# First four k tiles in smaller loads from two queues, last products in two column halves, output in quarter rows

## The chip, the cores and the metric

The kernel runs on one core of one Trainium2 chip. The metric is device time in microseconds (us) of one launch, from the program's start to its end; lower is better. Times are medians of several runs. The profile is one further execution taken by the hardware profiler, with times counted from the start of its span.

Engines in what follows: PE is TensorE (matrix products), PEld its weight loads, DVE is VectorE, ACT is ScalarE, POOL is GpSimd, SP is SyncE, which here only issues transfers. A "q" behind an engine (SPq, ACTq) means its instruction sequencer, for instance when it issues a DMA.

## The reference

Two pre-norm residual layers over a stream of 256 tokens by 2048 features, float32, batch 1, and a final RMSNorm:

```python
def reference(x, norm_mix, norm_ffn, norm_final, w_in_even, w_out_even, swa_sinks,
              mlstm_b_i, mlstm_b_f, mlstm_head_gain, w_in_odd, fox_b_f, w_out_odd,
              w_gate, w_up, w_down):
    h = x
    for layer in range(DEPTH):          # DEPTH = 2
        j = layer // 2
        xn = rms_norm(h, norm_mix[layer])
        if layer % 2 == 0:
            mix = swa_mlstm_mixer(xn, w_in_even[j], w_out_even[j], swa_sinks[j],
                                  mlstm_b_i[j], mlstm_b_f[j], mlstm_head_gain[j])
        else:
            mix = forgetting_attention_mixer(xn, w_in_odd[j], fox_b_f[j], w_out_odd[j])
        h = h + mix.astype(h.dtype)
        h = h + swiglu(rms_norm(h, norm_ffn[layer]), w_gate[layer], w_up[layer], w_down[layer])
    return rms_norm(h, norm_final)

def rms_norm(x, g):
    xf = x.astype(jnp.float32)
    y = xf * lax.rsqrt(jnp.mean(xf * xf, axis=-1, keepdims=True) + RMS_EPS)
    return (y * g.astype(jnp.float32)).astype(x.dtype)

def swiglu(xn, w_gate, w_up, w_down):
    return (jax.nn.silu(xn @ w_gate) * (xn @ w_up)) @ w_down
```

Nearly all the work is matrix products of the 256 tokens with float32 weights. The change touches the first of these products (`xn @ w_in_even`, from its first tiles on) and the last (`... @ w_down` of the second layer, its last 512 output columns) with the final norm behind it.

## The kernel before

**A product.** Features lie on the partitions: D = 2048 features are KT = 16 k tiles of P = 128. The 256 tokens are two row tiles, t = 0 and 1, of 128. Output columns go in groups of NB = 512. Each float32 operand is split into a high part of reduced precision and the rest, and one product is three matmuls: high by high, high by the weights' rest, x's rest by high (L204 to L206). The x side (128 x 128) is the stationary operand, the weights (128 x 512) stream past it.

**Weights.** `load_raw` (L115) loads CK = 2 k tiles of 512 columns, 512 KB, in one DMA on SP into one of four `raw` buffers. `split_chunk` (L169) makes `hi` on ACT (L176) and `lo = raw - hi` on DVE (L177). `gemm` (L190) walks the k tiles of one column group: for each k, both row tiles, three matmuls each. In the last chunk group (`skew` chunks of 2 k tiles) it sorts by row tile, so that t = 0 ends first and its output work runs under the products of t = 1.

**The start** (L103 to L135 and L697 to L705). ACT issues a 32 KB load of the norm gains `gT` (L111); a one-element copy (L105) makes it load its function table. SP issues x, which is stored transposed as `xt`, into `xc` in five pieces (L127: k 0-1, 2-3, 4-7, 8-11, 12-15) with the first four weight loads between them. Meanwhile PE runs WARM = 3 rounds of four 128 x 128 float32 products on a constant (L135). Then, in four steps of four k tiles, ACT makes `xh = xc * gain` (L700), DVE makes the rest `xl` (L701), and `gemm` takes those k tiles into `acc0`.

**The end** (L643 to L648 and L1249 to L1272). In the last pass of the second layer the column groups n = 2 and n = 3 of `w_down` go through `gemm`, n = 3 with skew = 3, so that its last six k tiles run all for t = 0 and then all for t = 1: 18 matmuls of 512 columns for each. `finish` adds the sums to `h`, takes the sum of squares on ACT (L1256), and for n = 3 the mean on DVE (L1265) and the power -1/2 on POOL (L1266), scales the row tile (ACT the first 1024 columns, L1267; DVE the others, L1268 and L1269) and SP writes it out in two halves of 1024 columns (L1272).

**What sets the order.** A scheduler in the compiler places each engine's instructions by a simulated timeline; `tc.issue_after` adds an order by hand. Every DMA of SP and ACT takes one of eight completion semaphores (DMAHW0 to DMAHW7) in turn, and a DMA is issued only when the earlier one on its semaphore has landed. SP issues in program order, so a waiting DMA holds back those behind it.

Of the kernel before, what the change touches and what calls it, by code (L numbers as in the profile page):

```python
# [35 lines left out]
WARM = 3  # L36
# [28 lines left out]
def trunk(  # L65
# [45 lines left out]
    nc.scalar.dma_start(gT, gains)  # L111

# [19 lines left out]
    for _ in range(WARM):  # L132
        pw = pm.tile([P, 4, P], F32, tag="pm", name="pw")
        for i in range(4):
            nc.tensor.matmul(pw[:, i, :], ones, ones, start=True, stop=True)  # L135
# [26 lines left out]
    last_split = [None]  # L162
    last_mul = [None]

    def load_chunk(w, k0, c0, n):
        raw = ahead.pop(0) if ahead else load_raw(w, k0, c0, n)
        return split_chunk(raw, n)

    def split_chunk(raw, n):  # L169
        hi = wp.tile([P, CK, NB], F32R, tag="hi", name="hi")  # L170
        lo = wp.tile([P, CK, NB], F32R, tag="lo", name="lo")
        with ExitStack() as order:
            if behind[0]:
                order.enter_context(tc.issue_after(behind[0].ins))
                behind[0] = None
            latest[0] = nc.scalar.copy(hi[:, :, 0:n], raw[:, :, 0:n])  # L176
        nc.vector.tensor_tensor(  # L177
            out=lo[:, :, 0:n], in0=raw[:, :, 0:n], in1=hi[:, :, 0:n].bitcast(F32), op=ALU.subtract
        )
        return hi, lo  # L180
# [9 lines left out]
    def gemm(acc, lhs, w, c0, n, k_from, k_to, k_all, skew=1):  # L190
        k0 = k_from
        while k0 < k_to:
            last = k_to == k_all and k0 + skew * CK >= k_all
            chunks = [load_chunk(w, kc, c0, n) for kc in range(k0, k_all if last else k0 + CK, CK)]
            order = [(i, t) for i in range(len(chunks) * CK) for t in range(NT)]
            if last:
                order.sort(key=lambda it: it[1])
            for i, t in order:
                k = k0 + i
                hi, lo = (c[:, i % CK, 0:n] for c in chunks[i // CK])  # L200
                ah, al = lhs(k)
                ts = slice(t * P, (t + 1) * P)
                o = acc[t][:, 0:n]
                nc.tensor.matmul(o, ah[:, ts], hi, start=(k == 0), stop=False)  # L204
                nc.tensor.matmul(o, ah[:, ts], lo, start=False, stop=False)  # L205
                last_mm[0] = nc.tensor.matmul(o, al[:, ts], hi, start=False, stop=(k == k_all - 1))  # L206
            k0 += len(chunks) * CK
# [360 lines left out]
    def ffn(layer, fp, room, pending, sx, sd, key, idx_next=None, key_next=None, finish=None, then=None):  # L568
# [8 lines left out]
        for part, (g0, g1) in enumerate(zip(PARTS, PARTS[1:])):  # L577
# [64 lines left out]
            for n0 in (0, 2):  # L642
                if end and idx_next is None and n0 == 2:  # L643
                    for n in (2, 3):
                        acc = new_acc()
                        gemm(acc, m_of, wd, n * NB, NB, 0, nk, nk, skew=3 if n == 3 else 1)
                        close(acc, n)
                    continue  # L648
# [49 lines left out]
    for n in range(4):  # L698
        for k in range(4 * n, 4 * n + 4):
            nc.scalar.mul(xh[:, k, :], xc[:, k, :], gT[:, k : k + 1])  # L700
# [4 lines left out]
        gemm(acc0, x_of, wi, OFF_KS, NB, 4 * n, 4 * n + 4, KT)  # L705
# [540 lines left out]
    fs = cp.tile([P, NT, 4], F32, name="fs")  # L1246
    ft = cp.tile([P, 3, NT], F32, name="ft")

    def finish(acc, n, gf):  # L1249
        ns = slice(n * NB, (n + 1) * NB)  # L1250
        gn_ = gf[n // CK][:, n % CK, :]
        for t in range(NT):
            o = h[:, t, ns]
            nc.vector.tensor_tensor(out=o, in0=acc[t], in1=o, op=ALU.add)
            junk = sm.tile([P, NB], BF16, tag="junk", name="junk", bufs=1)
            nc.scalar.activation(junk, o, AF.Square, accum_out=fs[:, t, n : n + 1])  # L1256
# [8 lines left out]
            nc.vector.tensor_scalar(mean, fs[:, t, 3:4], 1.0 / D, part, op0=ALU.mult, op1=ALU.add)  # L1265
            nc.gpsimd.tensor_tensor(out=rs, in0=mean, in1=mhalf[:, 0:1], op=ALU.pow)  # L1266
            nc.scalar.mul(h[:, t, 0 : 2 * NB], h[:, t, 0 : 2 * NB], rs)  # L1267
            nc.vector.tensor_scalar(h[:, t, 2 * NB : 3 * NB], h[:, t, 2 * NB : 3 * NB], rs, None, op0=ALU.mult)  # L1268
            nc.vector.scalar_tensor_tensor(out=o, in0=o, scalar=rs, in1=gn_, op0=ALU.mult, op1=ALU.mult)  # L1269
            for half in (1, 0):  # L1270
                hs = slice(half * 2 * NB, (half + 1) * 2 * NB)
                nc.sync.dma_start(ov[:, t, hs], h[:, t, hs])  # L1272
# [51 lines left out]
```

## Time and profile before

| | us |
|---|---|
| median of 3 runs | 2087.18 |
| the three runs | 2086.15, 2087.18, 2089.94 |
| the profiled execution, its whole time | 2087.4 |
| its span | 2085.6 |
| PE busy within the span | 2074.6 |
| DVE busy | 1803.8 |
| ACT busy | 1378.9 |

The span is what the profiler recorded between the first and the last event; 1.8 us of the profiled execution lie around it. A row of a timeline gives the start in us, the length in us, the engine, the line of the kernel, the operation, the tiles (out<-in) and how many instructions were merged; what stands in brackets is the engine's idle time ahead of it and what ended it. Matmuls are pipelined, so one that is listed with 0.39 us follows the one before it after 0.23 us.

### The profile page before, as it was taken

How to read it: one execution, taken by the hardware profiler on the slowest of the kernel's cores; microseconds unless marked ns; L12 is line 12 of the kernel's file. 1: busy time of each engine (PE TensorE's matmuls, PEld its weight loads, DVE VectorE, ACT ScalarE, POOL GpSimd, SP SyncE). 2: the span in 40 equal slices, each digit the busy share in tenths (PEclk: the TensorE clock that was granted, in tenths of full speed). 3: DMA queues.
4: the chain of work that ended last, by engine and by line, in shares of the span. 5: the costliest groups of instructions: out<-in, count | busy, mean ns of one | idle time of the engine just before them, and what ended most of it. 6: DMA issues, size and time to landing. Idle time of an engine off the chain costs nothing.

```text
span 2085.6 us, 26737 instructions
## 1 busy us (share of the span) xinstructions
PE 2074.6 (99%) x9486; PEld 1723.5 (83%) x9486; DVE 1803.8 (86%) x2396; ACT 1378.9 (66%) x1733; POOL 51.6 (2%) x70
## 2 busy tenths in 40 slices
PE   9999999999999999999999999999999999999998
PEld 7888888888888888888888888888888888888886
DVE  6788868999999998998799776679999999999995
ACT  6577568666567656767867676687666567556763
POOL 2110000000000000000020000000000000000000
PEclk9999999999999999999999999999999999999999
DMA  9446767766676667666687675677767576757663
GB/s 332 125 142 184 247 193 228 240 198 205 211 228 214 214 195 220 212 220 176 200 261 207 199 212 169 197 231 231 231 194 229 187 230 201 239 177 226 219 205 125
DMA packets 308661, 435.61 MB, mean 209 GB/s; under 512 B 106272, under 2 KB 114480, under 8 KB 308528
## 3 DMA queue, kind: packets, MB, share of 16 engines
q1 hardware_dynamic: 306768, 428.10, 65.3%
q0 software_dynamic: 1616, 5.78, 0.9%
q8 instruction: 74, 1.21, 0.2%
q14 instruction: 59, 0.48, 0.1%
q10 hardware_dynamic: 144, 0.03, 0.0%
HBM read 408.67 MB, written 2.11 MB: 197 GB/s over the span
## 4 chain that ended last, share of the span: by engine, by line
PE 98%; DMA 1%; DVE 0%; ACT 0%; issue 0%; POOLq 0%; POOL 0%; SPq 0%; DVEq 0%; ACTq 0%
PE acc L427 20%; PE acc L428 20%; PE acc L429 20%; PE acc L205 5%; PE acc L206 5%; PE acc L204 5%; PE prod L427 5%; PE prod L428 5%; PE prod L429 5%; PE vacc L206 1%; PE vacc L204 1%; PE vacc L205 1%; PE p L333 1%; PE po L386 1%; PE pp L378 0%
## 5 line engine op out<-in xcount | busy, mean ns | idle before, releaser
L176 ACT CAST hi<-raw 128x1024 fp32r<-128x1024 f32 (+1 forms) x664 | 674.0, 1030 | 406.0 <-PE acc L429 239.7
L177 DVE TENSOR_TENSOR lo<-raw,hi 128x1024 fp32r<-128x1024 f32 (+1 forms) x664 | 786.0, 1199 | 139.3 <-ACT hi L176 137.5
L428 PE MATMUL acc<-lo,xh 128*128 128x512 f32 x1204 | 469.1, 390 | 0.0
L429 PE MATMUL acc<-hi,xl 128*128 128x512 f32 x1204 | 465.1, 389 | 0.0
L427 PE MATMUL acc<-hi,xh 128*128 128x512 f32 x1204 | 462.9, 390 | 0.2 <-DVE u L562 0.2
L427 PEld LDWEIGHTS acc<-hi,xh 128*128 128x128 f32 x1204 | 226.3, 188 | 48.2 <-DVE u L562 0.6
L429 PEld LDWEIGHTS acc<-hi,xl 128*128 128x128 f32 x1204 | 226.4, 188 | 47.2
L428 PEld LDWEIGHTS acc<-lo,xh 128*128 128x128 f32 x1204 | 226.4, 188 | 47.0
L428 PE MATMUL acc<-lo,mh 128*128 128x512 f32 x444 | 172.7, 389 | 0.0
L429 PE MATMUL acc<-hi,ml 128*128 128x512 f32 x444 | 171.4, 389 | 0.0
L427 PE MATMUL acc<-hi,mh 128*128 128x512 f32 x444 | 169.3, 389 | 0.0
L302 ACT CAST ht<-raw 128x1024 fp32r<-128x1024 f32 x94 | 98.7, 1050 | 56.4 <-DVE raw L542 19.0
L205 PE MATMUL acc<-lo,mh 128*128 128x512 f32 x320 | 125.8, 393 | 0.0
L302 ACT CAST ht<-t 128x1024 fp32r<-128x1024 f32 x94 | 98.9, 1052 | 40.3 <-PE prod L429 27.3
L204 PE MATMUL acc<-hi,mh 128*128 128x512 f32 x320 | 125.4, 396 | 0.0
L206 PE MATMUL acc<-hi,ml 128*128 128x512 f32 x320 | 124.1, 391 | 0.0
L303 DVE TENSOR_TENSOR lt<-raw,ht 128x1024 fp32r<-128x1024 f32 x94 | 114.9, 1222 | 4.3 <-ACT ht L302 4.0
L303 DVE TENSOR_TENSOR lt<-t,ht 128x1024 fp32r<-128x1024 f32 x94 | 114.9, 1222 | 1.6 <-ACT ht L302 1.3
L302 ACT CAST hi<-raw 128x512 fp32r<-128x512 f32 x112 | 69.2, 618 | 59.5 <-PE acc L429 47.3
L429 PEld LDWEIGHTS acc<-hi,ml 128*128 128x128 f32 x444 | 83.4, 188 | 17.3
L427 PEld LDWEIGHTS acc<-hi,mh 128*128 128x128 f32 x444 | 83.4, 188 | 17.3
L428 PEld LDWEIGHTS acc<-lo,mh 128*128 128x128 f32 x444 | 83.3, 188 | 17.3
(370 smaller groups left out, 3588.5 us busy)
## 6 DMA issues: line engine op xcount, KB each, us to landing
raw<-in_w_gate_dram SPq DMA_DIRECT2D x176, 512.0 KB, 4.6
raw<-in_w_up_dram SPq DMA_DIRECT2D x176, 512.0 KB, 4.7
raw<-in_w_down_dram SPq DMA_DIRECT2D x176, 512.0 KB, 5.0
raw<-in_w_in_odd_dram SPq DMA_DIRECT2D x88, 512.0 KB, 4.9
raw<-in_w_in_even_dram SPq DMA_DIRECT2D x64, 512.0 KB, 4.8
raw<-in_w_out_even_dram SPq DMA_DIRECT2D x32, 512.0 KB, 4.5
raw<-in_w_out_odd_dram SPq DMA_DIRECT2D x32, 512.0 KB, 4.7
raw<-in_w_in_odd_dram SPq DMA_DIRECT2D x8, 272.0 KB, 3.3
```

The lines of the kernel that those rows point to most:

```text
L176: latest[0] = nc.scalar.copy(hi[:, :, 0:n], raw[:, :, 0:n])
L177: nc.vector.tensor_tensor(out=lo[:, :, 0:n], in0=raw[:, :, 0:n], in1=hi[:, :, 0:n].bitcast(F32), op=ALU.subtract)
L204: nc.tensor.matmul(o, ah[:, ts], hi, start=(k == 0), stop=False)
L205: nc.tensor.matmul(o, ah[:, ts], lo, start=False, stop=False)
L206: last_mm[0] = nc.tensor.matmul(o, al[:, ts], hi, start=False, stop=(k == k_all - 1))
L302: last_split[0] = nc.scalar.copy(dst_h, src)
L303: nc.vector.tensor_tensor(out=dst_l, in0=src, in1=dst_h.bitcast(F32), op=ALU.subtract)
L333: nc.tensor.matmul(p1[:, jj, :], q_of(j, 1), k_of(j), start=True, stop=True)
L386: nc.tensor.matmul(po, v_of(j, 0), t0[:, j, :], start=True, stop=False)
L427: nc.tensor.matmul(o, ah, hi, start=start, stop=False)
L428: nc.tensor.matmul(o, ah, lo, start=False, stop=False)
L429: nc.tensor.matmul(o, al, hi, start=False, stop=stop)
```

## The change

At the start: the first four k tiles of weights come as four loads of 256 KB, one for each k tile, ahead of everything else on SP; x of k 0 and k 1 comes as two loads of 128 KB issued by ACT; x of k 2-3 and then of k 4-5 and 6-7 in 256 KB loads on SP. `split_chunk` splits those first weights one k tile at a time, and x is scaled in steps of 2, 2, 2, 2, 4 and 4 k tiles, with each step's scaling ordered behind the cast before it. The constant products ahead (WARM) go from 12 to 10.

At the end: for n = 3, row tile t = 1, the products of the last six k tiles go into two new PSUM tiles of 256 columns, first all for the left half, then all for the right, 36 matmuls of 256 columns in place of 18 of 512. What t = 1 had gathered before is added to `h` on its own, each half is added and squared by itself, and the row tile is scaled and written in four quarters of 512 columns, three on SP and one on ACT.

```diff
-WARM = 3
+WARM = 10
...
     nc.scalar.dma_start(gT, gains)
+    for k in range(CK):
+        nc.scalar.dma_start(xc[:, k, :], xt[:, k, :])
...
-    for k0, k1, ks in ((0, 2, (0,)), (2, 4, (2,)), (4, 8, (4, 6)), (8, 12, ()), (12, 16, ())):
+    firsts = []
+
+    def load_first(k0):
+        raw = wr.tile([P, CK, NB], F32, tag="raw", name="raw", bufs=4)
+        for a in range(CK):
+            k = k0 + a
+            load[0] = nc.sync.dma_start(raw[:, a, :], wi[k * P : (k + 1) * P, OFF_KS : OFF_KS + NB])
+        firsts.append(raw)
+        ahead.append(raw)
+
+    load_first(0)
+    nc.sync.dma_start(xc[:, 2:4, :], xt[:, 2:4, :])
+    load_first(2)
+    for k0, k1, ks in ((4, 6, (4,)), (6, 8, (6,)), (8, 12, ()), (12, 16, ())):
         nc.sync.dma_start(xc[:, k0:k1, :], xt[:, k0:k1, :])
         ahead += [load_raw(wi, k, OFF_KS, NB) for k in ks]
...
-    for _ in range(WARM):
-        pw = pm.tile([P, 4, P], F32, tag="pm", name="pw")
-        for i in range(4):
-            nc.tensor.matmul(pw[:, i, :], ones, ones, start=True, stop=True)
+    pw = pm.tile([P, 4, P], F32, tag="pm", name="pw")
+    for i in range(WARM):
+        nc.tensor.matmul(pw[:, i % 4, :], ones, ones, start=True, stop=True)
...
+        for a in range(parts):
+            ks = slice(a * CK // parts, (a + 1) * CK // parts)
+            with ExitStack() as order:
+                if parts > 1:
+                    order.enter_context(tc.issue_after(xh_made[len(xh_made) - parts + a].ins))
...
+                latest[0] = nc.scalar.copy(hi[:, ks, 0:n], raw[:, ks, 0:n])
+            nc.vector.tensor_tensor(
+                out=lo[:, ks, 0:n], in0=raw[:, ks, 0:n], in1=hi[:, ks, 0:n].bitcast(F32), op=ALU.subtract
+            )
...
+            if last and halves:
+                head = [it for it in order if it[1] < NT - 1]
+                end = [it[0] for it in order if it[1] == NT - 1]
+                order = head + [
+                    (i, NT - 1, half, a * n // 2, (a + 1) * n // 2, k0) for a, half in enumerate(halves) for i in end
+                ]
...
-    for n in range(4):
-        for k in range(4 * n, 4 * n + 4):
-            nc.scalar.mul(xh[:, k, :], xc[:, k, :], gT[:, k : k + 1])
+    for k0, k1 in ((0, 2), (2, 4), (4, 6), (6, 8), (8, 12), (12, 16)):
+        with ExitStack() as order:
+            if k0:
+                order.enter_context(tc.issue_after(latest[0].ins))
+            for k in range(k0, k1):
+                xh_made.append(nc.scalar.mul(xh[:, k, :], xc[:, k, :], gT[:, k : k + 1]))
...
+            pieces = 2 if halves and t == NT - 1 else 1
+            if pieces == 2:
+                o = h[:, t, n * NB : (n + 1) * NB]
+                nc.vector.tensor_tensor(out=o, in0=acc[t], in1=o, op=ALU.add)
+            for a in range(pieces):
+                w = NB // pieces
+                o = h[:, t, n * NB + a * w : n * NB + (a + 1) * w]
+                nc.vector.tensor_tensor(out=o, in0=halves[a] if pieces == 2 else acc[t], in1=o, op=ALU.add)
+                junk = sm.tile([P, NB], BF16, tag="junk", name="junk", bufs=1)
+                nc.scalar.activation(junk[:, 0:w], o, AF.Square, accum_out=fs[:, t, n + a : n + a + 1])
+                if n == 3:
+                    dst = mean if a == pieces - 1 else part
+                    nc.vector.tensor_scalar(dst, fs[:, t, 3 + a : 4 + a], 1.0 / D, part, op0=ALU.mult, op1=ALU.add)
...
-            nc.scalar.mul(h[:, t, 0 : 2 * NB], h[:, t, 0 : 2 * NB], rs)
-            nc.vector.tensor_scalar(h[:, t, 2 * NB : 3 * NB], h[:, t, 2 * NB : 3 * NB], rs, None, op0=ALU.mult)
-            nc.vector.scalar_tensor_tensor(out=o, in0=o, scalar=rs, in1=gn_, op0=ALU.mult, op1=ALU.mult)
-            for half in (1, 0):
-                hs = slice(half * 2 * NB, (half + 1) * 2 * NB)
-                nc.sync.dma_start(ov[:, t, hs], h[:, t, hs])
+            q = [h[:, t, a * NB : (a + 1) * NB] for a in range(4)]
+            qo = [ov[:, t, a * NB : (a + 1) * NB] for a in range(4)]
+            nc.scalar.mul(q[0], q[0], rs)
+            nc.vector.tensor_scalar(q[2], q[2], rs, None, op0=ALU.mult)
+            nc.scalar.mul(q[1], q[1], rs)
+            nc.vector.scalar_tensor_tensor(out=q[3], in0=q[3], scalar=rs, in1=gn_, op0=ALU.mult, op1=ALU.mult)
+            for a in (2, 0, 3):
+                nc.sync.dma_start(qo[a], q[a])
+            nc.scalar.dma_start(qo[1], q[1])
```

The order on SP at the start, before, with the semaphores on which a DMA waits (DMAHW0 is the one of `gT`, DMAHW1 that of the first x load):

```order
L127 DMA xc<-in_xt_dram 128x512
L117 DMA raw<-in_w_in_even_dram 128x2x512
L127 DMA xc<-in_xt_dram 128x512
L117 DMA raw<-in_w_in_even_dram 128x2x512
L127 DMA xc<-in_xt_dram 128x1024
L117 DMA raw<-in_w_in_even_dram 128x2x512 x2
L127 DMA xc<-in_xt_dram 128x1024 [waits DMAHW0_49]
L127 DMA xc<-in_xt_dram 128x1024 [waits DMAHW1_49]
```

The same place with the change (here DMAHW0 is `gT`, DMAHW1 and 2 the first two weight loads, DMAHW3 and 5 the two x loads of ACT, DMAHW4 x of k 2-3):

```order
L134 DMA raw<-in_w_in_even_dram 128x512 x2
L139 DMA xc<-in_xt_dram 128x512
L134 DMA raw<-in_w_in_even_dram 128x512 x2
L142 DMA xc<-in_xt_dram 128x512 [waits DMAHW0_49]
L119 DMA raw<-in_w_in_even_dram 128x2x512 [waits DMAHW1_49]
L142 DMA xc<-in_xt_dram 128x512 [waits DMAHW2_49]
L119 DMA raw<-in_w_in_even_dram 128x2x512 [waits DMAHW3_49]
L142 DMA xc<-in_xt_dram 128x1024 [waits DMAHW4_49]
L142 DMA xc<-in_xt_dram 128x1024 [waits DMAHW5_49]
```

Five loads are issued without a wait where there were seven, and six wait for an earlier landing where two did; one weight load and the last x load wait for the x that ACT issues.

ACT at the start, with the change; before, L113 was not there, and L700 and L176 came as 2 scalings, 1 cast of 1024 columns, 2, 1, 4, 2, 8:

```order
L111 DMA gT<-in_gains_dram 128x64
L105 ACT_TABLE_LOAD
L105 COPY warm<-warm 128x1
L113 DMA xc<-in_xt_dram 128x256 x2
L734 ACTIVATE xh<-xc,gT 128x256
L195 CAST hi<-raw 128x512
L734 ACTIVATE xh<-xc,gT 128x256
L195 CAST hi<-raw 128x512
L734 ACTIVATE xh<-xc,gT 128x256 x2
L195 CAST hi<-raw 128x512 x2
L734 ACTIVATE xh<-xc,gT 128x256 x2
L195 CAST hi<-raw 128x1024
```

The two x loads stand behind the table load and the copy on ACT, and casts and scalings now alternate tile by tile.

ACT at the end, with the change (before: for each row tile L1256 of 512 columns, then L1267 of 1024):

```order
L1297 ACTIVATE junk,fs<-h 128x512 [waits DVE_49,Activation_49]
L1312 ACTIVATE h<-h,ft 128x512 [waits Pool_49]
L1314 ACTIVATE h<-h,ft 128x512
L1297 ACTIVATE junk,fs<-h 128x256 [waits DVE_49,Activation_49]
L1318 DMA out_dram<-h 128x512 [waits Activation_49]
L1297 ACTIVATE junk,fs<-h 128x256 [waits DVE_49,Activation_49]
L1312 ACTIVATE h<-h,ft 128x512 [waits Pool_49]
L1314 ACTIVATE h<-h,ft 128x512
L1318 DMA out_dram<-h 128x512 [waits Activation_49]
```

The first row tile's output DMA of ACT stands between the two squares of the second row tile.

More of the change, by code (lines that the diff above doesn't have):

```diff
@@ L645, in ffn @@
                         acc = new_acc()
[L646 to L647 removed]
+                        halves = [pm.tile([P, NB // 2], F32, tag="pm", name="half") for _ in range(2)] if n == 3 else None
+                        gemm(acc, m_of, wd, n * NB, NB, 0, nk, nk, skew=3 if n == 3 else 1, halves=halves)
+                        if halves:
+                            finish(acc, n, gf, halves)
+                        else:
+                            close(acc, n)
                     continue
```

44 lines of the change are left out of this document (19 added, 25 removed).

## The prediction

> **What bounds the kernel now.** I read the page's totals and its chain of waits first, then the timeline of the first 20 us and of the last 10, since the change touches only these.
>
> ```profile
> span 2085.6 us, 26737 instructions
> PE 2074.6 (99%) x9486; PEld 1723.5 (83%) x9486; DVE 1803.8 (86%) x2396; ACT 1378.9 (66%) x1733; POOL 51.6 (2%) x70
> PE 98%; DMA 1%; DVE 0%; ACT 0%; issue 0%; POOLq 0%; POOL 0%; SPq 0%; DVEq 0%; ACTq 0%
> ```
>
> PE is busy for 2074.6 of 2085.6 us and is 98% of the chain that ended last. No product is removed, so the only time to be had lies where PE does no product: ahead of its first and behind its last. The start, by the timeline:
>
> ```profile
> 0.80 0.38 ACTq L111 DMA_DIRECT2D gT<-in_gains_dram  x1
> 1.10 5.34 PE L135 MATMUL pw<-ones 128*128 128x128 f32 x24 [1.10 <-POOL ones L131]
> 2.51 0.19 ACT L105 COPY warm<-warm 128x1 f32<-128x1 f32 x1
> 4.63 0.91 ACT L700 ACTIVATE xh<-xc,gT 128x256 fp32r<-128x256 f32 x2 [1.92 <-DMA xc<-in_xt_dram]
> 5.86 1.04 ACT L176 CAST hi<-raw 128x1024 fp32r<-128x1024 f32 x1 [0.32 <-DMA raw<-in_w_in_even_dram]
> 6.94 1.23 DVE L177 TENSOR_TENSOR lo<-raw,hi 128x1024 fp32r<-128x1024 f32 x1 [0.88 <-ACT hi L176]
> 6.96 0.73 PE L204 MATMUL acc<-hi,xh 128*128 128x512 f32 x2 [0.51 <-ACT hi L176]
> 8.22 0.50 PE L205 MATMUL acc<-lo,xh 128*128 128x512 f32 x1 [0.53 <-DVE lo L177]
> 9.75 1.71 ACT L700 ACTIVATE xh<-xc,gT 128x256 fp32r<-128x256 f32 x4 [0.21 <-DMA xc<-in_xt_dram]
> 11.37 2.15 ACT L176 CAST hi<-raw 128x1024 fp32r<-128x1024 f32 x2
> 12.43 2.36 DVE L177 TENSOR_TENSOR lo<-raw,hi 128x1024 fp32r<-128x1024 f32 x2
> 13.71 0.19 PEld L205 LDWEIGHTS acc<-lo,xh 128*128 128x128 f32 x1 [0.15 <-DVE lo L177]
> ```
>
> Landing, cast and subtraction of the first 512 KB follow one another: the weights land at 5.86, `hi` is done at 6.90, `lo` at 8.17. PE does two products at 6.96 and stands again until 8.22. The second thing to see is k 4: PE comes to it and at 13.71 waits 0.15 us more, for the `lo` that DVE began at 12.43, because x of k 4 to 7 landed only at 9.75. So what is won at k 0 counts only as far as k 4's `lo` comes before 13.7 as well.
>
> **The start, part by part.** Weights of one k tile land sooner than of two, and cast and subtraction are halved. But x of k 0 and 1 now comes from ACT, behind its copy, which ends at 2.70; one issue took 0.38 us there, so the two go out at 2.7 and 3.1. The trace has no such load. Its nearest rows are the DMA listing's (KB, us from issue to landing):
>
> ```profile
> gT<-in_gains_dram ACTq DMA_DIRECT2D x1, 32.0 KB, 3.5
> xc<-in_xt_dram SPq DMA_DIRECT2D x1, 256.0 KB, 3.7
> xc<-in_xt_dram SPq DMA_DIRECT2D x1, 256.0 KB, 4.8
> raw<-in_w_in_even_dram SPq DMA_DIRECT2D x1, 512.0 KB, 6.2
> DMA packets 757, 1.67 MB, mean 341 GB/s; under 512 B 58, under 2 KB 58, under 8 KB 757
> L176 ACT CAST hi<-raw 128x512 fp32r<-128x512 f32 x16 | 9.9, 618 | 10.6 <-PE acc L429 3.7 <-PE acc L206 3.2 <-PE vacc L206 2.1
> ```
>
> The first row was alone on its queue, the second first in its own, the third and fourth stood behind 768 KB and 1 MB. With 128 KB each, behind `gT` on one queue and beside SP's 1.28 MB on the other, I take 3.5 us for the first (x at 6.2, where before it was 4.63) and 4.0 for the second (7.1), nearer to 3.7 than to 4.8 for their size.
>
> ACT is then the chain. From x of k 1 it has five scalings at 0.43 (1.71 for four), the casts of k 1, 2 and 3 at about 0.6, one cast of 1.05, and DVE the `lo` of 1.23: 2.15 + 1.8 + 1.05 + 1.23 = 6.25 us. `lo` of k 4 is done at 7.1 + 6.25 = 13.35, against 13.66 (12.43 + 1.23) before: **0.3 us won**. PE agrees: scaling and cast of k 0 end at 6.2 + 1.0 = 7.2, `lo` at 7.9, the stream is as if begun at 7.45, and 4 k tiles of six products at 0.227 later it asks for that `lo` at 13.35. Behind it ACT has about 1.9 us of work for two k tiles and PE 2.7, so no later tile binds, as far as loads keep up.
>
> The bounds: were ACT's issues not held by the copy, they would go at 1.2 and 1.6 and land at 4.7 and 5.1 (3.5 each); PE's stream would begin at 5.95 and ask for k 4's `lo` at 11.85, and the loads would just allow it (2.2 MB moved by 8.8 in the window from 3.9, with 0.5 before it, of the 2.3 needed): 1.85 won. Were the second as late as the 512 KB row (6.2 from 3.1, landing at 9.3), `lo` would end at 15.55: 1.9 lost. SP's new waits matter through the same landing: x of k 12 to 15 is held until x of k 1 is there, with over 1 MB still queued ahead, which covers it; without that cover PE would wait at k 12, not before.
>
> [...]
>
> **The constant products** go from 12 to 10, that is from 24 rows to 20, and end at 1.10 + 20 x 0.2225 = 5.55 instead of 6.44. PE would stand in either case; cost 0 unless the clock is touched (a rival below).
>
> **The end.** The rows for matmuls of 256 columns, then the tail of t = 1, and the nearest rows for halved additions and squares:
>
> ```profile
> 99.32 0.28 PE L204 MATMUL acc<-hi,xh 128*128 128x256 f32 x1
> 100.27 0.28 PE L206 MATMUL acc<-hi,xl 128*128 128x256 f32 x1
> 2072.16 0.23 PE acc L204
> 2076.96 0.69 DVE L1254 TENSOR_TENSOR h<-acc,h 128x512 f32<-128x512 f32 x1 [0.48 <-PE acc L206]
> 2077.74 0.63 ACT L1256 ACTIVATE junk<-h 128x512 bf16<-128x512 f32 x1 [1.26 <-DVE h L1254]
> 2079.38 1.15 ACT L1267 ACTIVATE h<-h,ft 128x1024 f32<-128x1024 f32 x1 [0.91 <-POOL ft L1266]
> 2079.38 0.49 DVE L1268 TENSOR_SCALAR h<-h,ft 128x512 f32<-128x512 f32 x1 [0.67 <-POOL ft L1266]
> 2079.78 0.75 DVE L1269 SCALAR_TENSOR_TENSOR h<-h,ft,gf 128x512 f32<-128x512 f32 x1
> 2080.55 0.33 SPq L1272 DMA_DIRECT2D out_dram<-h  x1
> 2080.94 0.42 SPq L1272 DMA_DIRECT2D out_dram<-h  x1
> L497 DVE TENSOR_TENSOR h<-xh,xl 128x256 f32<-128x256 f32 x6 | 2.4, 414 | 0.0
> L971 ACT ACTIVATE junk<-hv 128x256 bf16<-128x256 f32 x8 | 3.3, 416 | 1.1 <-DVE hv L969 1.0
> ```
>
> Eight steps from 99.32 to 100.27 are 0.119 us each, weight loads hidden; 36 of them are 4.28 against 18 x 0.227 = 4.09: **+0.2**. The addition behind the last product shrinks from 0.69 to 0.41 and the square from 0.63 to 0.42: **-0.5**. Between the two squares ACT must scale t = 0 and issue a DMA: its scaling starts 4.05 ahead of 2079.38, at 2075.33, two halves of about 0.65 end at 2076.6, the left square at 2077.2, an issue of 0.38 at 2077.6, just when the right half is added (2076.96 + 0.2 + 0.41 = 2077.57): **+0.1** allowed. The scale factor is there 0.2 earlier, at 2079.18.
>
> From there the first output waits for one quarter only (0.49, issue at 2079.7) where it waited for two DVE steps (2080.55): 0.85 earlier. Three issues on SP at some 0.43 and one on ACT, behind 1.3 us of scaling, put the last one at about 2080.6 where it was 2080.94. One megabyte of output per row tile is the same, so the end comes between 0.35 (last issue) and 0.85 (first) earlier; a last load of half the size lands sooner, hence **-0.8** in all for the end. Bounds: -1.5 if the smaller last transfer saves its whole 0.65 (256 KB at 0.4 MB/us) as well; +0.3 if ACT's DMA delays the second square by a whole issue more and quarter rows, shorter pieces, move as much slower as is won.
>
> Sum: -0.3 - 0.8 = -1.1. The profiled execution took 2087.4, its span and 1.8 around it, so its changed form would be 2086.3; the median lies 0.2 below that execution, so I forecast **2086.1**.
>
> **The rivals.** (1) *x from ACT lands late, and the kernel is slower.* For it: 288 packets of ACT's queue behind the 144 of `gT` must take turns with SP's, and SP's weights were issued first. Against it: `gT` itself landed in 3.5 us in that company. It decides from a landing of k 1's x at 8.2 (`lo` of k 4 at 14.45, 0.8 late, the whole gain of the end); at 9.3 the sum is +1.9 - 0.8: 2088.3.
>
> (2) *The clock comes up late.* The grouped rows and windows:
>
> ```profile
> L135 PE MATMUL pw<-ones 128*128 128x128 f32 x24 | 5.3, 420 | 1.1 <-POOL ones L131 1.1
> L378 PE MATMUL pp<-ident,s 128*128 128x128 f32 x56 | 9.5, 273 | 0.0
> 149.50:152.90 3.40, 3.40 (x10) 2.62 (x9) 3.40 (x11) 1.52 (x2) 0.79 (x1) 0.50 0.01 4
> ```
>
> The constant products take 420 ns where the same shape takes 273 later, so PE starts slow, and the first real ones at 6.96 are fast; around 150 us, after small matmuls, the granted clock was 0.50 for 3.4 us. With the constant products ending at 5.55 and a pause to about 7.2, PE might be held at half speed for one such stretch more: half of 3.4, +1.7, 2087.8. Against it: in the trace the pauses of 0.5 us each before 8.2 did not take the clock back. [...]
>
> (3) *Loads come early*: the first bound, -1.85 - 0.8: 2084.5.
>
> (4) *The start does not change*, k 4's data deciding as before: only the end's -0.8, 2086.4.
>
> **How the numbers follow.** Forecast 0.45, with a range of its own of 2085.4 to 2086.9; rivals 0.14, 0.13, 0.16 and 0.12. The range must hold rivals 1 to 4 and the spread of the runs (3.8 us over three), of which stretches at half clock that fall differently can make 1.7 each way: 2083.2 to 2088.6. Some 0.2%, 4.2 us, is what a measurement of this kernel can tell from no change, so faster means under 2083.0: rival 3 with one slow stretch fewer, or a larger end, 0.16. Slower, above 2091.4, needs rivals 1 and 2 together with an unlucky run: 0.08. No change: 0.76.
>
> **What would show it.** Right: first product near 7.2 and none waiting over 0.3 us behind it, k 4's `lo` done near 13.35; last product 0.2 later than its place; first output of t = 1 issued some 0.5 us behind the scale factor. Wrong: x of k 1 landing above 8.2; products spaced 0.43 instead of 0.23 behind 7 us; quarter outputs that end no sooner than 4.7 us behind the first issue; or a wait in the middle, which nothing here foresees.

## The result, and the profile after

| | before | after |
|---|---|---|
| median, us | 2087.45 (5 runs, 2086.15 to 2089.94) | 2102.81 (5 runs, 2102.25 to 2104.64) |
| ratio, 95% interval | | 1.0073 (1.0062 to 1.0083) |
| span of the profiled execution, us | 2085.6 | 2101.1 |

(The five runs of before are the three shown above and two more.) The kernel became 15.4 us slower, where 2086.1 was forecast and 2088.6 was the end of the range. The totals of the page after, with PE's share of the chain of waits:

```profile
span 2101.1 us, 26796 instructions
PE 2090.5 (99%) x9500; PEld 1723.3 (82%) x9500; DVE 1807.0 (86%) x2401; ACT 1379.0 (66%) x1739; POOL 46.1 (2%) x70
PE 96%; DMA 1%; ACT 1%; DVE 1%; issue 1%; SPq 0%; POOLq 0%; POOL 0%; ACTq 0%; DVEq 0%
```

PE is busy 15.9 us longer (2090.5 against 2074.6) and stands no longer than before. So the loss is not a wait: PE took longer for the same products. Both ends of the kernel, where the prediction looked, are in order. The start, by the timeline:

```profile
0.81 0.41 ACTq L111 DMA_DIRECT2D gT<-in_gains_dram  x1
1.25 1.28 ACT L105 ACT_TABLE_LOAD   x1 [1.25 <-PEq L1351]
1.32 0.88 ACTq L113 DMA_DIRECT2D xc<-in_xt_dram  x2
5.00 0.51 ACT L734 ACTIVATE xh<-xc,gT 128x256 fp32r<-128x256 f32 x1 [2.26 <-DMA xc<-in_xt_dram]
6.07 0.73 PE L231 MATMUL acc<-hi,xh 128*128 128x512 f32 x2 [0.34 <-ACT hi L195]
7.39 0.51 ACT L734 ACTIVATE xh<-xc,gT 128x256 fp32r<-128x256 f32 x1 [1.37 <-DMA xc<-in_xt_dram]
8.46 0.73 PE L231 MATMUL acc<-hi,xh 128*128 128x512 f32 x2 [0.47 <-ACT hi L195]
12.03 1.23 DVE L196 TENSOR_TENSOR lo<-raw,hi 128x1024 fp32r<-128x1024 f32 x1
12.99 0.62 PE L231 MATMUL acc<-hi,xh 128*128 128x512 f32 x2
13.44 0.40 PE L232 MATMUL acc<-lo,xh 128*128 128x512 f32 x1
16.41 1.05 ACT L195 CAST hi<-raw 128x1024 fp32r<-128x1024 f32 x1 [0.93 <-DMA raw<-in_w_in_even_dram]
```

The first product came at 6.07 instead of 6.96, and k 4's `lo` was done at 13.26 where 13.35 was forecast. The end, from the addition behind the last product on:

```profile
2092.68 0.28 PE L233 MATMUL half<-hi,ml 128*128 128x256 f32 x1
2092.99 0.42 DVE L1295 TENSOR_TENSOR h<-half,h 128x256 f32<-128x256 f32 x1 [0.68 <-PE half L233]
2093.51 0.42 ACT L1297 ACTIVATE junk<-h 128x256 bf16<-128x256 f32 x1 [0.64 <-DVE h L1295]
2094.93 0.49 DVE L1313 TENSOR_SCALAR h<-h,ft 128x512 f32<-128x512 f32 x1 [0.67 <-POOL ft L1309]
2096.30 0.37 ACTq L1318 DMA_DIRECT2D out_dram<-h  x1
```

From the start of the last product to the end of the span it takes 2101.1 - 2092.68 = 8.42 us, where it was 2085.6 - 2076.53 = 9.07. The loss lies between. Of the windows view, one row of a stretch in the middle, before first (window, length, then busy us and number of instructions of PE, PEld, DVE, ACT, POOL, then the granted clock, DMA share and GB/s):

```profile
500.00:600.00 100.00, 100.00 (x443) 82.84 (x442) 95.49 (x120) 59.28 (x64) 0.00 (x0) 1.00 0.63 208
```

and the same row after:

```profile
500.00:600.00 100.00, 100.00 (x438) 81.94 (x437) 94.84 (x120) 58.58 (x64) 0.00 (x0) 1.00 0.63 207
```

PE is busy all the time at a granted clock of 1.00, and has 438 products in these 100 us instead of 443. That is what to see here: a busy share of 100% in both, and a different rate. The loss begins between 300 and 400 us: from 100 to 300 us both kernels do 981 products, in the next 100 us it is 443 before and 439 after. It goes on to the end. The timeline of PE alone shows where within a stretch. In a row such as `acc<-hi,mh` the first tile behind the arrow (`hi`) is the one that streams past, and the second (`mh`) is the stationary operand, called the left tile from here on. After:

```profile
1000.35 0.39 PE L454 MATMUL acc<-hi,mh 128*128 128x512 f32 x1
1000.58 0.39 PE L455 MATMUL acc<-lo,mh 128*128 128x512 f32 x1
1000.80 0.40 PE L456 MATMUL acc<-hi,ml 128*128 128x512 f32 x1
1001.04 0.62 PE L454 MATMUL prod<-ht,sd 128*128 128x512 f32 x2
1001.50 0.39 PE L455 MATMUL acc<-lo,mh 128*128 128x512 f32 x1
1001.73 0.40 PE L456 MATMUL acc<-hi,ml 128*128 128x512 f32 x1
1001.96 0.39 PE L454 MATMUL acc<-hi,mh 128*128 128x512 f32 x1
1002.19 0.39 PE L455 MATMUL acc<-lo,mh 128*128 128x512 f32 x1
```

Starts are 0.226 apart as a rule; from 1000.80, where the next product is the first with another left tile (`sd`), it takes 0.24, and the products behind the two with `sd` are 0.23 apart for a while. In the kernel before, the product ahead of such a change of tiles takes 0.23 (1004.78 to 1005.01) and the one with `sd` 0.22 (1005.01 to 1005.23):

```profile
1004.55 0.39 PE L428 MATMUL acc<-lo,mh 128*128 128x512 f32 x1
1004.78 0.39 PE L429 MATMUL acc<-hi,ml 128*128 128x512 f32 x1
1005.01 0.39 PE L427 MATMUL acc<-hi,sd 128*128 128x512 f32 x1
1005.23 0.62 PE L427 MATMUL prod<-ht,sd 128*128 128x512 f32 x2
1005.69 0.39 PE L427 MATMUL acc<-hi,mh 128*128 128x512 f32 x1
```

Taken over all products between 300 and 2050 us (start of one to start of the next, those 220 to 250 ns apart, less 226.65 ns), by the tile that a product streams and by the left tile of the product behind it, which PE loads meanwhile (in the changed kernel the 0.19 us load of `ml` starts at 1000.58, with the product `acc<-lo,mh` ahead of it):

```
streams  next left tile   pairs        extra ns each     us in all
                       before after    before  after    before after
hi, lo   xh xl mh ml     5573  5505      0.11   1.31      0.6   7.2
hi, lo   sx sd            595   595      0.03   6.29      0.0   3.7
ht, lt   xh xl mh ml      535   535      0.02   5.94      0.0   3.2
ht, lt   sx sd            593   593      0.00   2.18      0.0   1.3
```

With some 160 pairs of other tiles it is 16.3 us after and 0.8 before: the 15.5 us of the spans. (By 2050 us the changed kernel has got less far, hence its fewer pairs.) `xh`, `xl`, `mh`, `ml` hold the high and low parts of x or of the activations; `sx` and `sd` hold those of sums of such tiles, which some of the layers' products take in their place, and `ht` and `lt` those of the weights combined in the same way. The first product with `sx` starts at 344.7 us in the kernel before, in the 100 us in which the loss begins.

What sets the two kinds apart is where they lie. One line of the diff that is not printed above is this:

```diff
-    fs = cp.tile([P, NT, 4], F32, name="fs")
+    fs = cp.tile([P, NT, 5], F32, name="fs")
```

`fs` takes 32 bytes of each partition before, and 40, rounded up to 64, after. Every tile allocated behind it starts 32 bytes later. Start addresses in the built programs (bytes within a partition; raw(w) are the buffers of `load_raw`):

```
tile                     xh     hi     lo    raw(w)   sx0     sd0     ht
before                  4224  69760  94336  118912  155520  167808  212864
after                   4224  69760  94336  118912  155552  167840  212896
before, modulo 256       128    128    128     128     128     128     128
after, modulo 256        128    128    128     128     160     160     160
```

A product reads a slice of such a tile, and the slices of these tiles begin at multiples of 512 bytes within them, so the start of the tile modulo 256 is that of every operand cut from it.

### The profile page after: what moved, and what is told of

It is laid out like the page before. It is cut to its first block, busy times and chain, and to the rows that moved or that the text cites. A ratio compares the mean times of both kernels' runs of the same rounds, so it can differ in the third digit from the quotient of the medians.

```text
span 2101.1 us, 26796 instructions
## 1 busy us (share of the span) xinstructions
PE 2090.5 (99%) x9500; PEld 1723.3 (82%) x9500; DVE 1807.0 (86%) x2401; ACT 1379.0 (66%) x1739; POOL 46.1 (2%) x70
## 4 chain that ended last, share of the span: by engine, by line
PE 96%; DMA 1%; ACT 1%; DVE 1%; issue 1%; SPq 0%; POOLq 0%; POOL 0%; ACTq 0%; DVEq 0%
PE acc L454 20%; PE acc L456 20%; PE acc L455 20%; PE prod L454 5%; PE prod L456 5%; PE acc L232 5%; PE prod L455 5%; PE acc L233 5%; PE acc L231 5%; PE vacc L232 1%; PE vacc L233 1%; PE vacc L231 1%; DMA raw<-in_w_in_even_dram 1%; PE p L360 1%; PE po L413 0%
## 5 line engine op out<-in xcount | busy, mean ns | idle before, releaser
L195 ACT CAST hi<-raw 128x1024 fp32r<-128x1024 f32 (+3 forms) x666 | 674.3, 1027 | 422.2 <-PE acc L456 255.7
L196 DVE TENSOR_TENSOR lo<-raw,hi 128x1024 fp32r<-128x1024 f32 (+3 forms) x666 | 783.9, 1191 | 148.6 <-ACT hi L195 146.1
```

Of the source, the lines that this page charges most:

```text
L195: latest[0] = nc.scalar.copy(hi[:, ks, 0:n], raw[:, ks, 0:n])
L196: nc.vector.tensor_tensor(out=lo[:, ks, 0:n], in0=raw[:, ks, 0:n], in1=hi[:, ks, 0:n].bitcast(F32), op=ALU.subtract)
```

## The experiments

**Addresses or instructions?** Four kernels: the kernel before with nothing but the moved tiles, the changed kernel without moving them, and both with a move of 64 bytes.

The kernel before with the wider `fs`:

```diff
-    fs = cp.tile([P, NT, 4], F32, name="fs")
+    fs = cp.tile([P, NT, 5], F32, name="fs")
```

> The kernel before, with nothing changed but `fs`, which has 5 columns instead of 4; it computes the same, and the fifth column is never used. Every tile placed behind `fs` (ht, lt, sx, sd, the heads and more) starts 32 bytes later, as in the changed kernel. Theory A (the loss comes from where those tiles start: products that read one of them and one that did not move take 5 to 7 ns longer each): about 2103 us, 15.5 above before (the whole 2102.8 - 2087.4, with no start and end to subtract perhaps 1 more), products spaced 228.9 ns on average between 300 and 2050 us where before has 226.75, and the pairs (hi, next sx) and (ht, next xh) some 6 to 7 ns up. Theory B (the loss comes from the change's own instructions, the queues and half tiles): 2087 us and 226.75 ns.

Measured: 2103.83 us, ratio to before 1.0083 (1.0069 to 1.0097). Its row of the windows view:

```profile
500.00:600.00 100.00, 100.00 (x438) 81.91 (x438) 94.45 (x120) 58.93 (x64) 0.00 (x0) 1.00 0.64 206
```

An unused column gives the whole loss; the rate is the changed kernel's, and so are the pairs (hi, next sx) with 6.92 ns and (ht, next xh) with 6.27.

The changed kernel with the fifth sum kept elsewhere:

```diff
-    fs = cp.tile([P, NT, 5], F32, name="fs")
-    ft = cp.tile([P, 3, NT], F32, name="ft")
+    fs = cp.tile([P, NT, 4], F32, name="fs")
+    ft = cp.tile([P, 4, NT], F32, name="ft")
...
-                nc.scalar.activation(junk[:, 0:w], o, AF.Square, accum_out=fs[:, t, n + a : n + a + 1])
+                nc.scalar.activation(junk[:, 0:w], o, AF.Square, accum_out=ft[:, 3, 0:1] if a else fs[:, t, n : n + 1])
```

> The changed kernel with `fs` at 4 columns again: the fifth sum of squares stands in a fourth row of `ft`, which fits without moving a tile behind it. All else of the change is there. Theory A: the loss is gone, and what is left is what the start and the end give: 2085.5 to 2086.5 us (the sum of the prediction, -1.1, or a little more as the first product came at 6.07), products at 226.75 ns. Theory B: 2102 to 2103 us and 228.9 ns.

Measured: 2086.94 us, ratio 1.0002 (0.9993 to 1.001).

```profile
span 2085.2 us, 26796 instructions
500.00:600.00 100.00, 100.00 (x443) 82.84 (x442) 96.04 (x121) 58.89 (x64) 0.00 (x0) 1.00 0.64 207
```

All of the change's instructions are there and the loss is gone. Together the two runs settle that addresses make the loss and the new instructions none of it. The time itself came out at the level of the kernel before and not in the 2085.5 to 2086.5 us expected; the interval of its ratio would still hold a gain of 1.1 us (0.9995). The terms are taken up further down.

The kernel before with 64 bytes:

```diff
-    fs = cp.tile([P, NT, 4], F32, name="fs")
+    fs = cp.tile([P, NT, 12], F32, name="fs")
```

> The kernel before with `fs` of 12 columns, of which 4 are used: every tile behind it starts 64 bytes later. Theory A with a period of 64 bytes (what counts is the start modulo 64): 2087.4 us, as before, 226.75 ns. Rival C (any other start than before's costs, or the period is 128): some 2095 to 2105 us, with the same pairs slow. Theory B: 2087.4 us too.

Measured: 2100.86 us, 1.0065 (1.0053 to 1.0078). And the changed kernel with the same 12 columns:

> The changed kernel with `fs` of 12 columns, of which 5 are used: the tiles behind it start 64 bytes later than before, 32 later than in the changed kernel. Theory A with a period of 64 bytes: the loss is gone, 2085.5 to 2086.5 us, the same as with the fifth sum in `ft`. Rival C: 2095 to 2105 us. Theory B: 2102 to 2103 us.

Measured: 2099.96 us, 1.0065 (1.0053 to 1.0078). A period of 64 bytes is refuted; rival C holds in both, with a loss somewhat smaller than for 32 bytes (the sum of the extra is 13.1 us in both, against 16.3).

**Which starts count?** Theory A1 at this point was that a product loses when the start of what PE reads changes from one product to the next, A2 that each read off a certain boundary is slow. Four kernels move different groups of tiles of the kernel before. First everything by 32 bytes:

```diff
+    ctx.enter_context(tc.tile_pool(name="pad", bufs=1)).tile([P, 8], F32, name="pad")
     sp_ = ctx.enter_context(tc.tile_pool(name="split", bufs=1))
```

> The kernel before with 32 unused bytes ahead of everything, so that all tiles, xh, hi and lo as well as sx, ht and lt, start 32 bytes later and stand to each other as before. Theory A1 (a product loses time when the start of what TensorE reads, modulo 128 or more bytes, changes from one product to the next): no loss, 2087 us and 226.75 ns a product. Theory A2 (each read of a tile that doesn't start on a multiple of 128 bytes is slow in itself): more tiles are off than in the changed kernel, so at least its 16 us, over 2103 us.

Measured: 2087.69 us, 1.0001 (0.9992 to 1.0011).

```profile
500.00:600.00 100.00, 100.00 (x443) 82.80 (x442) 95.58 (x121) 59.54 (x65) 0.00 (x0) 1.00 0.64 208
```

All operands start at 160 modulo 256 and nothing is lost: A2 falls. What is left that can count is how tiles stand to each other. Then the tiles ahead of `cp` by 128 bytes:

```diff
+    c0 = ctx.enter_context(tc.tile_pool(name="c0", bufs=1))
+    sink = c0.tile([P, SWA_H], F32, name="sink")
+    bias_f = c0.tile([P, FOX_H], F32, name="bias_f")
     sp_ = ctx.enter_context(tc.tile_pool(name="split", bufs=1))
...
-    sink = cp.tile([P, SWA_H], F32, name="sink")
-    bias_f = cp.tile([P, FOX_H], F32, name="bias_f")
```

> The kernel before with two small tiles (sink and bias_f, 128 bytes together) allocated ahead of the others: xh, xl, mh, ml, hi, lo and raw start 128 bytes later, the tiles of the layers (sx, sd, ht, lt) where they were. Period of 128 bytes: no loss, 2087 us, 226.75 ns. Period of 256 bytes or more: a loss of the order of the 13.5 us that a relative shift of 64 bytes cost, 2095 to 2105 us, in the same pairs (hi, next sx) and (ht, next xh).

Measured: 2102.13 us, 1.0072 (1.0055 to 1.0088); (hi, next sx) 6.94 ns, (ht, next xh) 5.98. The period is not 128.

Then `sd`, `ht`, `lt` and the rest of the layers' tiles by 32 bytes, with `sx` left in place:

```diff
     sx = [late.tile([P, len(mixed_of(ORDER)), 4, P], F32R, name=f"sx{i}") for i in range(2)]
+    late.tile([P, 8], F32, name="pad")
```

> The kernel before with 32 unused bytes behind sx: sx stays, and the tiles of the layers behind it (sd, ht, lt, heads) start 32 bytes later. Theory A1: the pairs (hi, next sx) and (lo, next sx), 6.9 and 4.6 ns up with all moved, are free unless a product of ht or lt is close ahead; (ht, next xh) and (hi, next sd) stay 6 to 7 ns up, and products of ht with sx, free of a change when both moved, now become slow too. In all some 10 to 16 us: 2097 to 2103 us. If only the tiles at the left of a product counted (sx, sd: the ones that are loaded ahead): some 3 to 4 us, by the share of the pairs with sd; if only those streamed (ht, lt): about as with all moved, 2102 us.

Measured: 2101.68 us, 1.0066 (1.0051 to 1.0081). Extra ns by pair, beside those with all moved:

```
pair (streams, next left)    hi,sx   hi,sd   ht,xh   ht,sx   lt,sx   mh,sx
32 bytes, all of them         6.92    6.65    6.22    1.85    2.29    5.89
32 bytes, sx left in place    1.33    6.70    6.13    7.72    6.22    0.10
```

Each pair behaves as its own two tiles stand: with `sx` back at `hi`'s start (hi, sx) is nearly free and (ht, sx), which had been level, is slow. This also rules out that only the streamed or only the loaded tile counts: (hi, sd) is slow though `hi` did not move, and (ht, sx) is slow though `sx` did not.

Last, `xh`, `xl`, `mh`, `ml` by 32 and `hi`, `lo`, `raw` by 128 bytes:

```diff
+    c0 = ctx.enter_context(tc.tile_pool(name="c0", bufs=1))
+    mhalf = c0.tile([P, 8], F32, name="mhalf")
     sp_ = ctx.enter_context(tc.tile_pool(name="split", bufs=1))
...
+    c1 = ctx.enter_context(tc.tile_pool(name="c1", bufs=1))
+    bias_g = c1.tile([P, 8], F32, name="bias_g")
+    sink = c1.tile([P, SWA_H], F32, name="sink")
     wp = ctx.enter_context(tc.tile_pool(name="wp", bufs=6))
...
-    mhalf = cp.tile([P, 8], F32, name="mhalf")
-    bias_g = cp.tile([P, 8], F32, name="bias_g")
-    sink = cp.tile([P, SWA_H], F32, name="sink")
```

> The kernel before with 32 bytes of small tiles ahead of xh, xl, mh and ml, and 96 more behind them: these four tiles, which TensorE loads as the left side of most products, start 32 bytes later, hi, lo and raw 128 later, the rest where it was. Theory A1 with a period of 128: loss only where a product with xh or mh follows or precedes one with sx or sd, 3 to 10 us: 2090 to 2097 us. If what counts is the start of the left tile against that of the streamed one: all 6900 products with xh, xl, mh or ml lose, 1 to 7 ns each, 2095 to 2135 us. If only the streamed tiles count: 2087 us.

Measured: 2140.14 us, 1.0252 (1.0237 to 1.0267), 52 us slower.

```profile
500.00:600.00 100.00, 100.00 (x431) 80.57 (x430) 93.55 (x118) 57.17 (x63) 0.00 (x0) 1.00 0.61 201
```

```profile
1499.72 0.40 PE L430 MATMUL acc<-lo,xh 128*128 128x512 f32 x1
1499.96 0.40 PE L431 MATMUL acc<-hi,xl 128*128 128x512 f32 x1
1500.19 0.40 PE L429 MATMUL acc<-hi,xh 128*128 128x512 f32 x1
1500.42 0.40 PE L430 MATMUL acc<-lo,xh 128*128 128x512 f32 x1
1500.66 0.40 PE L431 MATMUL acc<-hi,xl 128*128 128x512 f32 x1
```

The first row is of the windows view, 431 products; the others are of the timeline, with starts 0.23 to 0.24 apart. `xh` and `xl` start alike, `hi` and `lo` start alike, nothing changes from one product to the next, and yet they lose 6.6 to 7.8 ns on average, by pair of tiles, and 6.0 to 7.9 in long stretches without any other tile. A1 falls, and its 2090 to 2097 us with it; the other reading, left tile against streamed tile, had put its upper end at 2135.

**The theory that is left (A3), and the period.** A product is slow when the tile that it streams and the left tile that is loaded meanwhile for the next product start at different places modulo some period. The first run moves all tiles ahead of `cp` by 256 bytes:

```diff
+    c0 = ctx.enter_context(tc.tile_pool(name="c0", bufs=1))
+    gT = c0.tile([P, 4 * KT], F32, name="gT")
     sp_ = ctx.enter_context(tc.tile_pool(name="split", bufs=1))
...
-    gT = cp.tile([P, 4 * KT], F32, name="gT")
```

> The kernel before with gT (256 bytes) allocated ahead of the others: xh, xl, mh, ml, hi, lo and raw start 256 bytes later, the layers' tiles where they were. Theory A3 (a product is slow when the tile it streams and the tile that is loaded meanwhile for the next product differ in their start modulo the period) with a period of 256 bytes: no loss, 2087 us, 226.75 ns a product. With a longer period, or with a table of distances that has no period: 2095 to 2105 us, as for 32, 64 and 128.

Measured: 2087.85 us, 1.0004 (0.9995 to 1.0014).

```profile
500.00:600.00 100.00, 100.00 (x443) 82.78 (x442) 95.57 (x120) 59.29 (x64) 0.00 (x0) 1.00 0.65 208
```

No loss: this shift of 256 bytes cost nothing, 443 products in the 100 us as before. The second is the counterpart of the 52 us run: the streamed tiles are moved, the left ones stay:

```diff
+    c1 = ctx.enter_context(tc.tile_pool(name="c1", bufs=1))
+    mhalf = c1.tile([P, 8], F32, name="mhalf")
     wp = ctx.enter_context(tc.tile_pool(name="wp", bufs=6))
...
-    mhalf = cp.tile([P, 8], F32, name="mhalf")
```

> The kernel before with one tile of 32 bytes (mhalf) ahead of hi, lo and raw: these, and the small tiles up to mhalf, start 32 bytes later, xh, xl, mh, ml and all of the layers' tiles (sx, sd, ht, lt) where they were. Theory A3: every product that streams hi or lo meets a loaded tile of another start, as in the run that moved xh, so 2130 to 2145 us, the pairs (hi, next xh) 6 to 7 ns up in long stretches too; only products that stream ht or lt are free. Rival (what counts is the start of the loaded tile alone, which was off in the slow runs with sx, sd or xh moved): no loss here, 2087 us.

Measured: 2137.32 us, 1.0244 (1.0228 to 1.026).

```profile
500.00:600.00 100.00, 100.00 (x431) 80.55 (x430) 93.69 (x117) 54.94 (x60) 0.00 (x0) 1.00 0.62 199
```

The time is as A3 had it, and the start of the left tile alone does not decide. One part of the expectation failed: the pairs that are level in this run are not free, (ht, next sx) shows 4.93 ns and (ht, next xh) 3.95; such pairs mostly stand between slow ones (below).

All runs so far in one table, starts modulo 256:

```
                          xh..ml  hi,lo,raw   sx   sd,ht,lt      us
before                      128      128     128     128       2087
all by 32                   160      160     160     160       2087.7
first tiles by 256          128      128     128     128       2087.9
change, sum in ft           128      128     128     128       2086.9
change                      128      128     160     160       2102.8
before, fs of 5             128      128     160     160       2103.8
before, fs of 12            128      128     192     192       2100.9
change, fs of 12            128      128     192     192       2100.0
layer's tiles by 32         128      128     128     160       2101.7
first tiles by 128            0        0     128     128       2102.1
x tiles by 32, w by 128     160        0     128     128       2140.1
w tiles by 32               128      160     128     128       2137.3
```

**The change's own two parts**, each alone and without moved tiles. The start:

> The changed kernel's start alone (smaller first loads, two queues, 20 constant products), with the end of the kernel before and `fs` of 4 columns. By the prediction's term -0.3 us: 2087.1; by the trace of the changed kernel with the fifth sum in `ft`, whose products ran 0.3 us ahead at 50 us: the same, 2087.1. If the smaller loads cost more than they bring: over 2088.5 us.

Measured: 2087.45 us, 1.0003 (0.9994 to 1.0012). Its edit is the diff of the change without what it does in the last pass and in `finish`, `fs` at 4 columns; the constant products are the change's ten, which are 20 rows in the trace. The end alone is the rest of the diff, with the fifth sum in `ft`:

> The changed kernel's end alone (column halves of the last products, quarter outputs, the fifth sum in `ft`), with the start of the kernel before. By the prediction's term -0.8 us: 2086.6; by the trace of the run with the whole change but the shift, whose tail was about 0.3 us shorter: 2087.0. If the halves and the smaller outputs cost more than they bring: over 2088.5 us.

Measured: 2086.34 us, 0.9998 (0.999 to 1.0007). Neither part can be told from no change by its time, nor from the -0.3 and -0.8 us forecast for it, and no version here is faster than the kernel before beyond the noise.

## Why the prediction was wrong

**The step that failed** is its first: "the change touches only these", the first 20 us and the last 10, and from it that "the only time to be had lies where PE does no product: ahead of its first and behind its last". That no product is removed was taken to mean that the products keep their pace. The diff had a line that allocates, the widened `fs`, and it was given no cost at all; it moved the operands of the layers' products by 32 bytes, and that made 15.5 us between 300 and 2050 us. No view of the profile before could have priced it, since all its pairs are level (0.00 to 0.11 ns). The last sentence on what would show it, "a wait in the middle, which nothing here foresees", looked at the right place for the wrong sign: there was no wait, PE's share of busy time was the same, and only its number of products per 100 us told.

Point by point, the rest:

- **x from ACT was not held by the copy.** The two loads were issued from 1.32 on, while the table load ran (1.25 to 2.53), not at 2.7 and 3.1. So the condition of rival 3 came true. But the x of k 1 took until 7.39, where that bound had 5.1, and 7.1 was forecast. Landing, not issue, set it (5.62 us from 1.74 on in the chain of waits); why it took so much longer than the 3.6 us of the x of k 0 was not tried. Rival 1 would have needed 8.2.
- **k 4's `lo`** was done at 13.26 (forecast 13.35; the four parts of that sum add up to 6.23 us, not 6.25, and PE asks for this `lo` behind 26 products, not 24). PE reached k 4 at 12.99 and took that `lo` at 13.44, where it was 13.82 before: 0.38 won, where 0.3 was forecast.
- **"No later tile binds, as far as loads keep up"** is the step of the -0.3 that failed: they did not keep up. The cast of k 8 waited 0.93 us for its load at 16.41, and at 35 us PE stood for a `lo` whose weights had landed late:

```profile
33.30 1.05 ACT L195 CAST hi<-raw 128x1024 fp32r<-128x1024 f32 x1 [4.32 <-DMA raw<-in_w_in_even_dram]
35.67 0.19 PEld L232 LDWEIGHTS acc<-lo,xh 128*128 128x128 f32 x1 [0.67 <-DVE lo L196]
35.67 0.50 PE L232 MATMUL acc<-lo,xh 128*128 128x512 f32 x1 [0.25 <-DVE lo L196]
```

The two products ahead of and at this wait took 0.98 us (35.03 to 36.01) instead of 0.45, so 0.53 was lost and the 0.38 of k 4 with it. All four profiled kernels with the new start have such a gap near 35 us, and none with the old start has one. At 50 to 100 us the ACT and DVE instructions that both kernels share stood 0.15 us behind those of before in the changed kernel, 0.28 ahead in the one with the sum in `ft`, 0.20 behind in the start alone. What the start is worth in the end is not settled to 0.3 us by this: kernels with the old start stood between 0.59 ahead (the end alone) and 1.40 behind (all tiles by 32) at the same place.
- **A second issuer.** x of k 0, issued by ACT at 1.32, was there at 5.00, later than the 4.63 of before, and 3.6 us behind its issue where the first x load of before, twice its size, took 3.7. No run here tries a second issuer by itself, so what it is worth alone is not shown.
- **The clock** (rival 2) did not come up late: where PE does not wait, products from 7 us on are 0.23 apart. The half-clock stretch at 150 us is there as before, 10 products in 3.40 us (first row). But in one profile such a stretch fell on the start: in the kernel with all tiles moved by 32 bytes, whose start is that of before, the granted clock was 0.51 from 8.50 to 11.90 (second row), with 9 products where the kernel before has 16. That is enough for its 1.40 us.

```profile
149.30:152.70 3.40, 3.40 (x10) 2.66 (x9) 3.40 (x11) 1.44 (x2) 0.87 (x1) 0.50 0.04 16
8.50:11.90 3.40, 3.40 (x9) 2.64 (x9) 2.77 (x6) 3.15 (x6) 0.00 (x0) 0.51 1.05 413
```

- **The end.** In the kernel with the sum in `ft`, by its timeline:

```profile
2072.60 0.28 PE L231 MATMUL half<-hi,mh 128*128 128x256 f32 x1
2076.79 0.28 PE L233 MATMUL half<-hi,ml 128*128 128x256 f32 x1
2079.05 0.48 DVE L1313 TENSOR_SCALAR h<-h,ft 128x512 f32<-128x512 f32 x1 [0.67 <-POOL ft L1309]
2080.41 0.37 ACTq L1318 DMA_DIRECT2D out_dram<-h  x1
```

The 36 half products cost what was forecast (2076.79 + 0.12 - 2072.60 = 4.31, forecast 4.28). From the first of these products to the scale factor it takes 6.45 us, where the same stretch was 2079.38 - 2072.68 = 6.70: 0.25 won, forecast 0.2. The outputs are the term that was mis-sized. The forecast had the end between 0.35 us (by the last issue) and 0.85 us (by the first) earlier, the 0.2 of the scale factor included, and took 0.8 because a last transfer of half the size would land sooner. It did not: from the last output's issue to the end of the span it is 4.7 us before and here. From the scale factor to the end of the span it was some 6.3 us before and is 6.15 here (5.96 in the end alone, 2084.6 - 2078.64). In sum the end brought 0.3 to 0.6 us in these profiles. Even this is not firm to some tenths: in the start alone, whose end is that of before, the same stretch behind the scale factor took 6.8 us.

So without the moved tiles the kernel was level with the one before within what its runs can tell. In the profiles the end's -0.8 was too large by 0.2 to 0.5, and the changed start's -0.3 was won at k 4 and lost again at 35 us; by the run times alone neither term is refuted. With the moved tiles the kernel is 0.73% slower, by a mechanism that was on no list of rivals.

## What to carry to other kernels

Read an edit for what it allocates as well as for what it computes. For products like these (128 x 512, float32 operands): list the start addresses of the matmul operands of both versions, and treat any that moved against the others as a likely cost in all of PE's stretches: here moves that left differences of 32, 64, 96 or 128 bytes cost some 13.5 to 52 us, and one of 256 bytes none (2087.85 us). Put a small new tile into the slack of another (in `ft` 24 of 32 bytes were taken, and the fifth sum fitted into the rest) or pad it so that the big operands keep their starts. And in a kernel that is bound by PE look at the number of products in equal windows, since the rows of 500 to 600 us above say 100.00 busy for the kernel before (443 products), for the one 0.7% slower (438) and for the one 2.5% slower (431).

## What the runs showed of the hardware

Not expected: in these runs PE's pace went with how the streamed tile and the left tile loaded meanwhile stood to each other in the partition. For 128 x 512 products at a granted clock of 1.00, starts that agree modulo 256 bytes gave 226.75 ns a product (three layouts: before, all tiles by 32, the first by 256), and differences of 32, 64, 96 and 128 bytes were all slower, by 6 to 8 ns a product on average in the two runs in which every product that streams `hi` or `lo` has a left tile of another start.

In the kernel before there are 9486 loads of 187 ns on average for 9486 products, and the 128 x 512 products are 226.75 ns apart with a load under every one of them. In the 52 us run, also with a load under every product, they are 233 ns apart on average.

That it is the next product's left tile which counts is seen at the entry to a group: after at least 12 products with level tiles, the product ahead of the first one with `sx` or `sd` takes 8.35 ns longer in the changed kernel (121 cases; 0.05 before), whether that next product streams `hi`, `lo` or `ht`, `lt`; the slow product itself has level tiles. The run that left `sx` in place makes it sharper: there the product ahead of `sd` takes the same 8.35 ns longer (38 cases), and the one ahead of `sx` 0.1 (83 cases). Behind the last odd tile the extra fades over some nine products (5.4, 5.3, 2.9, 4.6, 3.7, 1.9, 1.8, 0.8, 0.2 ns, then under 0.1), although those are level: that is most of the 7.2 us on pairs of `hi`, `lo` with `xh` to `ml`, almost half of the loss. Why it takes so many was not tried.

Open: the price by distance. With 64 bytes the entry costs nothing (0.8 ns less than usual), and the products behind it lose all the same; with 128 bytes the entry takes 5.8 ns. So there is no one price for a pair, A3 says which layouts are slow but not how much each product loses, and why such layouts are slow is not shown. Shifts beyond those tried, other widths and other types are unknown.
